# Ten weight tiles of its own and a second PSUM bank for the first stage of a decoder step

## The chip, the cores and the metric

The kernel runs on one core of a Trainium2 chip. The metric is the device time of one execution in microseconds; the time of a kernel is the median of its runs.

## What is computed

A step of a two-layer hybrid decoder on 256 prompt tokens and 8 sequences of 8 sample tokens (320 columns in all), all in fp32. Layer 0 mixes tokens by a gated MLP with a position-mixing matrix, layer 1 by a Mamba-2 scan; each is followed by a squared-ReLU MLP. Every sub-layer is normalised and then shifted and scaled by adaLN values, which are a projection of a conditioning vector. The first stage of the kernel covers the first lines of this cut:

```python
mod = (silu(c) @ ada_w[i] + ada_b[i]).reshape(c.shape[0], N_MOD, D_MODEL)
h = modulate(rms_norm(x, norm1_g[i]), mod[:, 0], mod[:, 1])   # h * (1 + scale) + shift
z = gelu(h @ w_in)
u, v = z[..., :D_GM], layer_norm(z[..., D_GM:], ln_g, ln_b)
...
y = (u * s) @ w_out
x = x + mod[:, 2][:, None, :] * y
h = modulate(rms_norm(x, norm2_g[i]), mod[:, 3], mod[:, 4])
x = x + mod[:, 5][:, None, :] * sq_relu_mlp(h, mlp_w1[i], mlp_w2[i])
```

D_MODEL is 1024, D_GM 2048; `c` holds 9 conditioning vectors (one for the prompt, eight for the samples).

## The kernel before

Activations lie with the model dimension on the partitions: `x`, `hhi` and `hlo` have 8 slices (`KD`) of 128 x 320. Every matrix product is made of three fp32r products: a weight tile is split into a high part `whi` (ScalarE, L135) and a low part `wlo` (VectorE, L136), the activations into `hhi` and `hlo`, and high x high, high x low and low x high are summed in PSUM. The split tiles rotate through three buffers each (`NHI`). Weights come in tiles of 128 x 1024 (512 KB), by SP's queue, into a ring `raw` of six (`NRAW`, L112) that all stages share.

The first stage (loop at L431) runs over the 8 slices `kt`. For each slice it makes the adaLN values of that slice and then adds the slice's part of the first half of `v = h @ w_in` to all its output tiles, in six PSUM banks that stay open through the loop (`acc0`, L424: three of the ring `mm`, the bank `nrm`, two of the three of the ring `ax`). In the order of the code a slice does this:

- it asks for the two halves of the next adaLN weights (`ada0`, L433), while the two of this slice, asked for a turn earlier, are used;
- L437: the adaLN product of a slice, for each half four matmuls of 128 x 32 against 128 x 256, each run as two instructions, so 8 instructions a half, summed in a bank from `ada_ps()` (L432), a ring of one;
- L445: load and split of the weights `gm_wv0` of the slice;
- L447: ScalarE copies the product out of PSUM; L450: four closing instructions on TensorE fold it and write it into the same bank; L453, L454: VectorE adds the bias and makes shift `md` and scale `am`;
- L456 to L463 and `norm_k` (L263): normalised, modulated and split slice `hhi`, `hlo`, and `hs` for the sample columns;
- `v_mm` (L407): 16 matmuls of 512 columns (L411 to L415).

At the end `v_out` (L417) takes the gelu of the six banks. The second stage (L471) does the same for the other half of `v`, with weights `gm_wv` through `wload` (L139). From there on each `wload` also takes a step of `ada_unit` (L152), which makes the adaLN values that later layers need: one load of `ada_w` (L156) and 8 instructions of L158, into the bank of `ada_ps()`. The projections of `u` and the rest of the kernel follow.

The norm of `x` at the start (L381 to L391) goes beside the first slices: its sum over the partitions is L210 on TensorE, its broadcast L205.

No order of instructions is written by hand across engines. A planner that simulates the program writes the order of each engine and of each DMA queue when the kernel is built; it takes what is ready and has a free buffer, earlier code first. So a load of a later stage can stand ahead of loads of this one on SP's queue. On the chip each engine and queue goes through its list in order, and waits at an instruction whose semaphores are not there yet.

Of the kernel before, what the change touches and what calls it, by code (L numbers as in the profile page):

```python
# [7 lines left out]
F32 = mybir.dt.float32  # L8
# [7 lines left out]
P = 128  # L16
# [6 lines left out]
T = TP + TS  # L23
# [15 lines left out]
NFIN = 5  # L39
MO = 6  # L40
NRAW = 6
NHI = 3
OFFS = (0, P, T - P)

# [7 lines left out]
def tile_trunk(ctx: ExitStack, tc: tile.TileContext, io):  # L52
# [14 lines left out]
    def nm(s):  # L67
        uid[0] += 1
        return f"{s}{uid[0]}"
# [3 lines left out]
    x = const.tile([P, KD, T], F32, name="x")  # L73
# [26 lines left out]
    def mm_ps():  # L100
        return psm.tile([P, 512], F32, tag="mm", name=nm("mm"))

    def ax_ps():
        return psx.tile([P, 512], F32, tag="ax", name=nm("ax"))

    def ada_ps():
        return psa.tile([P, 512], F32, tag="ada", name=nm("adap"))

    def nrm_ps():
        return psn.tile([P, 512], F32, tag="nrm", name=nm("nrm"))  # L110

    def raw_tile():  # L112
        return wp.tile([P, 8 * P], F32, tag="raw", name=nm("raw"), bufs=NRAW)

# [3 lines left out]
    b1 = lambda v: v.rearrange("p (b t) -> p b t", t=LS)  # L118
    bb = lambda v: v.unsqueeze(2).to_broadcast([P, NB, LS])

    # ---------------------------------------------------------------- weight stream and adaLN blocks
    fill = {"q": [], "rate": 0.0, "n": 0.0, "done": set()}

    def step():
# [7 lines left out]
    def split(raw, n=8 * P, eng=dve):  # L132
        hi = wp.tile([P, 8 * P], F32R, tag="whi", name=nm("whi"), bufs=NHI)
        lo = wp.tile([P, 8 * P], F32R, tag="wlo", name=nm("wlo"), bufs=NHI)
# [48 lines left out]
            dve.scalar_tensor_tensor(amul[2 * l + f // 3], md, 1.0, vec[:, g0 : g0 + 8].unsqueeze(2).to_broadcast([P, KD, 9]), ADD, MUL)  # L183
        fill["done"].add((l, f))

    # ---------------------------------------------------------------- norms
    def neg_rsqrt(r, v, a):
        dve.tensor_scalar(r.bitcast(I32), v.bitcast(I32), -0.5, 1597463007.0, MUL, ADD)
        for _ in range(3):
# [111 lines left out]
            act.activation(ghi[:, m, TP:T], t1, AF.Copy)  # L301
            pool.tensor_tensor(glo[:, m, TP:T], t1, ghi[:, m, TP:T].bitcast(F32), SUB)

    # ---------------------------------------------------------------- projections
    def mm3(ps, w, kk, hi, lo, first, last, n=T):
        whi, wlo = w
        pe.matmul(ps[:, :n], lhsT=whi[:, kk, :], rhs=hi, start=first, stop=False)  # L307
# [35 lines left out]
    def new_pool(side, bufs=1):  # L343
        c = ExitStack()
        return c, c.enter_context(tc.tile_pool(name=nm("pl"), bufs=bufs, side=side, reuse_waits="tile"))
# [29 lines left out]
        c.close()  # L375
        return ng

    # ---------------------------------------------------------------- layer 0 mixer
    fill["q"] = [ada_unit(l, f) for l in range(2) for f in range(6) if (l, f) not in ((0, 0), (0, 1), (1, 5))]
    act.activation(zero, zero, AF.Sqrt)  # L380
    for k in range(KD):  # L381
# [25 lines left out]
    def v_mm(pp, pq, whi, wlo, k):  # L407
        f, e = k == 0, k == KD - 1
        for c in range(2):
            sl = slice(c * P, (c + 1) * P)  # L410
            pe.matmul(pp[c], lhsT=hhi[:, k, sl], rhs=whi, start=f, stop=False)  # L411
            pe.matmul(pp[c], lhsT=hhi[:, k, sl], rhs=wlo, start=False, stop=False)  # L412
            pe.matmul(pp[c], lhsT=hlo[:, k, sl], rhs=whi, start=False, stop=e)  # L413
        pe.matmul(pq, lhsT=hs[:, k, :], rhs=whi, start=f, stop=False)
        pe.matmul(pq, lhsT=hs[:, k, :], rhs=wlo, start=False, stop=e)  # L415
# [6 lines left out]
        act.copy(vx[:, cs], pq)  # L422

    acc0 = [([mm_ps(), mm_ps()], ax_ps()), ([mm_ps(), nrm_ps()], ax_ps())]  # L424
    def load(src):
        raw = raw_tile()
        nc.sync.dma_start(raw, src)
        return raw

    nxt = [load(io["ada0"][0, hf]) for hf in range(2)]  # L430
    for kt in range(KD):  # L431
        ps = ada_ps()  # L432
        now, nxt = nxt, [load(io["ada0"][kt + 1, hf]) for hf in range(2)] if kt < KD - 1 else []  # L433
        for hf in range(2):
            raw = now[hf]
            for j in range(4):
                pe.matmul(  # L437
                    ps[32 * j : 32 * j + 32, :256],
                    lhsT=sc[:, 4 * hf + j, :],
                    rhs=raw[:, j * 256 : (j + 1) * 256],  # L440
                    start=(hf == 0),
                    stop=(hf == 1),
                    skip_group_check=True,
                )
        whi, wlo = split(load(io["gm_wv0"][kt]))  # L445
        sb = scratch()
        act.copy(sb[:, :256], ps[:, :256])  # L447
        pt = ps
        for i in range(2):
            pe.matmul(pt[:, 16 * i : 16 * i + 10], lhsT=sb[:, i * P : (i + 1) * P], rhs=cst[:, C_SS : C_SS + 10], start=True, stop=True, skip_group_check=True)  # L450
        for i in range(2):
            f = 8 * i + kt
            dve.tensor_scalar(md[:, f, :], pt[:, 16 * i : 16 * i + 9], vec[:, V_AB + f : V_AB + f + 1], None, ADD)  # L453
        dve.tensor_scalar(am[:, kt, :], md[:, 8 + kt, :], 1.0, vec[:, V_N1 + kt : V_N1 + kt + 1], ADD, MUL)  # L454
        t0 = tp.tile([P, TS], F32, tag="rs", name=nm("rs"))
        pool.tensor_tensor(b1(t0), b1(x[:, kt, TP:]), bb(am[:, kt, 1:9]), MUL)  # L456
        pool.tensor_tensor(t0, t0, r0[:, TP:], MUL)
        pool.tensor_tensor(b1(t0), b1(t0), bb(md[:, kt, 1:9]), ADD)
        act.activation(hhi[:, kt, TP:], t0, AF.Copy)
        dve.tensor_tensor(hlo[:, kt, TP:], t0, hhi[:, kt, TP:].bitcast(F32), SUB)  # L460
        norm_k(kt, am, md, r0)
        act.activation(hs[:, kt, 0:TS], t0, AF.Copy)
        act.activation(hs[:, kt, TS:], hlo[:, kt, TP:].bitcast(F32), AF.Copy)  # L463
        for j in range(2):
            cs = slice(512 * j, 512 * (j + 1))
            v_mm(*acc0[j], whi[:, cs], wlo[:, cs], kt)
    for j in range(2):
        v_out(j, *acc0[j])

# [80 lines left out]
    for m in range(KD):  # L550
        ps = proj1([io["gm_wo"][m, kc] for kc in range(2)], lambda k: uhi[:, k, :], lambda k: ulo[:, k, :])
        residual(ps, m, gate, g)
    uc.close()

    # ---------------------------------------------------------------- layer 0 mlp
    fill["rate"] = RATE1
    gc2 = []

# [5 lines left out]

    g = mlp(0, gc, g, nxt0)

    # ---------------------------------------------------------------- layer 1 mixer
    need(1, 4)
    fill["rate"] = 0.0
    r0 = rstd_x()  # L570
# [17 lines left out]
    ps = scaled(pss[0], r0)  # L588
# [52 lines left out]
        return st, bc, ea  # L641

    def ssd(g_, st, bc, ea, B, C, X, Z):
        # masked C.B^T and decays
        pc = ax_ps()
        for c in range(3):
            pe.matmul(pc[:, cq[c]], lhsT=B[:, OFFS[c] : OFFS[c] + P], rhs=C[:, cq[c]], start=True, stop=True, skip_group_check=True)
# [7 lines left out]
        dve.tensor_tensor(bc, bc, cbm.unsqueeze(1).to_broadcast([P, HG, T]), MUL)  # L655

        yield
        # token-major B and x
        Bd = dup(B, "dup0")
        Xd = [dup(X[r], f"dup{r + 1}") for r in range(2)]  # L660
        pB = ada_ps()
# [33 lines left out]
        dve.scalar_tensor_tensor(f2(xst), f2(xq), mrow(0), f2(xst).bitcast(F32), MUL, ADD)  # L695

        yield
        # prompt states
        pS = ax_ps()
        for c in range(2):  # L700
            pe.matmul(pS[:, c * GW : (c + 1) * GW], lhsT=Bn[:, c, :], rhs=xe[:, c, :], start=True, stop=True, skip_group_check=True)
# [4 lines left out]
        dve.tensor_tensor(fin, fin, pS[:, GW:], ADD)  # L706
        nc.gpsimd.dma_start(io["o_sp"][g_], fin)

        # terms of the entering states
        cp = mt([P, HG, P], "cp")  # L710
        cps = mt([P, NB, HG, LS], "cps")
        dve.tensor_tensor(cp, ea[:, :, :P], C[:, P:TP].unsqueeze(1).to_broadcast([P, HG, P]), MUL)
# [2 lines left out]
        for b in range(NB):  # L715
            j, hf = b % 4, b // 4
# [4 lines left out]
                start=True,  # L721
                stop=True,
# [3 lines left out]
        dve.tensor_tensor(ym, po.rearrange("p (c w) -> p c w", c=2), cst[:, C_DM : C_DM + GW].unsqueeze(1).to_broadcast([P, 2, GW]), MUL)  # L726

        yield
        # outputs of the scan
        Y = yt([P, 2, T], "Y")  # L730
        for r in range(2):
            py = ax_ps()
# [9 lines left out]
            for hf in range(2):  # L742
# [4 lines left out]
                    start=False,  # L747
                    stop=True,
# [4 lines left out]
        pool.tensor_tensor(Y, Y, Z, MUL)  # L753

        yield
        # gated group norm
        q0 = Z
        act.activation(q0, Y, AF.Square)
        q1 = scratch()
# [4 lines left out]
            dve.scalar_tensor_tensor(yst[m // 8][:, m % 8, :], Y[:, r], vec[:, V_NG + m : V_NG + m + 1], pr, MUL, MUL)  # L764

        yield
        # new sample states
        dec = ea[:, :, P:].rearrange("p h (b t) -> p b h t", t=LS)[:, :, :, LS - 1 : LS].to_broadcast([P, NB, HG, HD])
        pool.tensor_tensor(st.rearrange("p b (h e) -> p b h e", e=HD), st.rearrange("p b (h e) -> p b h e", e=HD), dec, MUL)
        for i in range(4):  # L770
# [24 lines left out]
    raw, dt, acm, stk, t1, t2, t3 = (yst[1][:, i, :] for i in range(7))  # L795
# [126 lines left out]
    acc["ring"] = nrm_ps  # L922
    yc.close()

    # ---------------------------------------------------------------- layer 1 mlp, final norm
    fill["q"].append(ada_unit(1, 5))
    fill["rate"] = 0.5
    mlp(1, gc, g, lambda: need(1, 5))
# [153 lines left out]
```

## Time and profile before

| | us |
|---|---|
| runs | 1133.29, 1131.8, 1141.0 |
| median | 1133.29 |
| span of the profiled execution | 1132.3 |

The span of the profiled execution goes from its first to its last instruction. The page gives busy time by engine: TensorE's matmuls 95% of the span, VectorE 62%, ScalarE 45%, GpSimd 35%. A matmul's busy time includes its way through the array, which overlaps that of the next, so these 95% are not TensorE at its peak; an idle time of TensorE is what counts. Of a wait the profile names who ended it, by the semaphore that came last. "PEclk" is the share of TensorE's full clock that was granted.

### The profile page before, as it was taken

To read this page: it belongs to the slowest core of one execution; us is meant where nothing else is said; L and a number is where in the kernel's file an instruction comes from. 1 tells how busy PE (TensorE), PEld (TensorE's weight loads), DVE (VectorE), ACT (ScalarE), POOL (GpSimd) and SP (SyncE) were. 2 spreads that over 40 slices of the span, in tenths; PEclk is the share of its full clock that TensorE was granted. 3 is DMA by queue.
4 is the path that set the end of the run, shared out by engine and by line. 5 is a ranking of instruction groups with operands and counts; after the bars stand their busy time and mean duration, and the time that the engine had idled before them with its cause. 6 is when DMAs were issued, how large, how long until landed. Compare 5 with 4: busy or idle time off the path is not lost.

```text
span 1132.3 us, 19072 instructions
## 1 busy us (share of the span) xinstructions
PE 1078.2 (95%) x7457; PEld 978.7 (86%) x7457; DVE 702.7 (62%) x1120; ACT 513.4 (45%) x899; POOL 395.3 (35%) x456
## 2 busy tenths in 40 slices
PE   5999999999999999999897999989999999999996
PEld 4667888889988898999895888888889999999996
DVE  3544856436644433446998999998976674443332
ACT  4443333435544433335773555554525555543331
POOL 1200124332333302223777666656423433320111
PEclk9999999999999999999998999998999999999998
DMA  9867785675767766445363555554345565444421
GB/s 342 295 224 248 272 299 166 208 245 183 233 213 223 220 211 222 149 149 181 98 206 115 191 190 182 183 183 137 132 157 188 173 232 165 150 151 149 149 94 47
DMA packets 60874, 213.92 MB, mean 189 GB/s; under 512 B 6560, under 2 KB 12128, under 8 KB 58480
## 3 DMA queue, kind: packets, MB, share of 16 engines
q1 hardware_dynamic: 58544, 200.47, 53.9%
q0 software_dynamic: 1952, 11.98, 2.8%
q8 instruction: 58, 0.95, 0.3%
q10 hardware_dynamic: 288, 0.26, 0.1%
q14 instruction: 32, 0.26, 0.1%
HBM read 199.31 MB, written 12.85 MB: 187 GB/s over the span
## 4 chain that ended last, share of the span: by engine, by line
PE 68%; DVE 18%; DMA 4%; issue 4%; POOL 2%; ACT 2%; SPq 0%; POOLq 0%; DVEq 0%; ACTq 0%
PE mm L307 18%; PE mm L309 17%; PE mm L308 17%; DVE co L615 5%; PE adap L158 4%; DVE wlo L136 2%; DVE nv L192 1%; PE mm L411 1%; PE mm L412 1%; DMA raw<-w_in 1%; PE mm L413 1%; PE ax L774 1%; PE ax L307 1%; ACT whi L135 1%; PE ax L308 1%
## 5 line engine op out<-in xcount | busy, mean ns | idle before, releaser
L136 DVE TENSOR_TENSOR wlo<-raw,whi 128x1024 fp32r<-128x1024 f32 (+1 forms) x221 | 272.3, 1233 | 216.9 <-ACT whi L135 216.0
L135 ACT ACTIVATE whi<-raw 128x1024 fp32r<-128x1024 f32 (+1 forms) x243 | 255.1, 1050 | 320.1 <-PE mm L308 213.8
L307 PE MATMUL mm<-hhi,whi 128*128 128x320 f32 x952 | 305.5, 321 | 2.3 <-ACT cb L608 1.8
L308 PE MATMUL mm<-hlo,whi 128*128 128x320 f32 x952 | 299.8, 315 | 1.3 <-DVE hlo L276 1.3
L309 PE MATMUL mm<-hhi,wlo 128*128 128x320 f32 x952 | 299.8, 315 | 1.3 <-DVE wlo L136 0.8
L307 PEld LDWEIGHTS mm<-hhi,whi 128*128 128x128 f32 x952 | 181.8, 191 | 20.4 <-issue 12.7
L308 PEld LDWEIGHTS mm<-hlo,whi 128*128 128x128 f32 x952 | 182.3, 191 | 3.4 <-DVE hlo L276 1.6
L309 PEld LDWEIGHTS mm<-hhi,wlo 128*128 128x128 f32 x952 | 181.6, 191 | 3.9 <-DVE wlo L136 1.4
L307 PE MATMUL mm<-mhi,whi 128*128 128x320 f32 x512 | 159.1, 311 | 0.0
L309 PE MATMUL mm<-mhi,wlo 128*128 128x320 f32 x512 | 158.1, 309 | 0.0
L308 PE MATMUL mm<-mlo,whi 128*128 128x320 f32 x512 | 157.9, 308 | 0.0
L358 POOL TENSOR_TENSOR ta<-ta 128x320 f32<-128x320 f32 x64 | 81.5, 1275 | 142.3 <-ACT ta L356 126.8
L307 PEld LDWEIGHTS mm<-mhi,whi 128*128 128x128 f32 x512 | 96.1, 188 | 4.1 <-issue 4.1
L308 PEld LDWEIGHTS mm<-mlo,whi 128*128 128x128 f32 x512 | 96.1, 188 | 0.0
L309 PEld LDWEIGHTS mm<-mhi,wlo 128*128 128x128 f32 x512 | 96.1, 188 | 0.0
L293 POOL TENSOR_TENSOR x<-x,rs 128x64 f32<-128x64 f32 x28 | 12.0, 430 | 226.5 <-DVE rs L292 226.5
L615 DVE SCALAR_TENSOR_TENSOR co<-cb,vec,co 128x344 f32<-128x344 f32 x96 | 82.3, 867 | 1.7 <-ACT co L613 1.2
L360 DVE TENSOR_TENSOR mlo<-ta,mhi 128x320 fp32r<-128x320 f32 x64 | 34.7, 547 | 53.6 <-ACT mhi L359 53.6
L359 ACT ACTIVATE mhi<-ta 128x320 fp32r<-128x320 f32 x64 | 30.1, 470 | 79.1 <-POOL ta L358 79.1
L136 POOL TENSOR_TENSOR wlo<-raw,whi 128x1024 fp32r<-128x1024 f32 x22 | 56.3, 2559 | 21.5 <-ACT whi L135 21.2
L158 PE MATMUL adap<-raw,sc 128*32 128x256 f32 x640 | 53.2, 392 | 0.9 <-DMA raw<-ada_w 0.9
L290 DVE SCALAR_TENSOR_TENSOR x<-mm,mod,x 128x256 f32<-128x256 f32 x29 | 14.0, 483 | 48.2 <-PE mm L309 46.8
(344 smaller groups left out, 1833.8 us busy)
## 6 DMA issues: line engine op xcount, KB each, us to landing
raw<-mlp_w SPq DMA_DIRECT2D x128, 512.0 KB, 3.9
raw<-ada_w SPq DMA_DIRECT2D x80, 512.0 KB, 4.4
raw<-w_in SPq DMA_DIRECT2D x48, 512.0 KB, 3.5
raw<-ada SPq DMA_DIRECT2D x16, 512.0 KB, 5.9
raw<-gm_wv SPq DMA_DIRECT2D x16, 512.0 KB, 6.2
raw<-gm_wu SPq DMA_DIRECT2D x16, 512.0 KB, 5.4
raw<-gm_wo SPq DMA_DIRECT2D x16, 512.0 KB, 4.5
st<-state SPq DMA_DIRECT2D x8, 1024.0 KB, 5.7
```

The costliest lines, as they stand in the source:

```text
L135: act.activation(hi[:, :n], raw[:, :n], AF.Copy)
L136: eng.tensor_tensor(lo[:, :n], raw[:, :n], hi[:, :n].bitcast(F32), SUB)
L158: pe.matmul(ps[32 * j : 32 * j + 32, :256], lhsT=sc[:, k, :], rhs=r[:, j * 256 : (j + 1) * 256], start=(k == 0), stop=(k == KD - 1), skip_ ...
L290: dve.scalar_tensor_tensor(x[:, m, :TP], ps[:, :TP], gate[:, m, 0:1], x[:, m, :TP], MUL, ADD)
L293: (dve if m == KD - 1 else pool).tensor_tensor(x[:, m, TP:], x[:, m, TP:], t0, ADD)
L307: pe.matmul(ps[:, :n], lhsT=whi[:, kk, :], rhs=hi, start=first, stop=False)
L308: pe.matmul(ps[:, :n], lhsT=whi[:, kk, :], rhs=lo, start=False, stop=False)
L309: pe.matmul(ps[:, :n], lhsT=wlo[:, kk, :], rhs=hi, start=False, stop=last)
L358: pool.tensor_tensor(s, t, t, MUL)
L359: act.activation(mhi[:, m, :], s, AF.Copy)
L360: dve.tensor_tensor(mlo[:, m, :], s, mhi[:, m, :].bitcast(F32), SUB)
L615: dve.scalar_tensor_tensor(o[:, :CO], cb[:, k : k + CO], wv(k), o[:, :CO], MUL, ADD)
```

## The change

- A pool of its own on the right side of SBUF holds ten tiles of 128 x 1024 for the first stage (`NRAW0`). Both the `ada0` and the `gm_wv0` loads of that stage go there, and no longer into the shared ring `raw` of six. The pool closes at the end of the stage.
- The adaLN product of a slice goes to the bank of `ada_ps()` for odd slices and to the third bank of the ring `ax` for even ones.
- The halves of a slice are multiplied in the order 1, 0, so the first matmul waits for the half that is asked for second, and `start` and `stop` change places.

Nothing is added to or taken from what is loaded or computed. Headings in comments are also left out.

```diff
@@ -39,6 +39,7 @@
 NRAW = 6
+NRAW0 = 10
 NHI = 3
...
@@ -422,24 +423,26 @@
     acc0 = [([mm_ps(), mm_ps()], ax_ps()), ([mm_ps(), nrm_ps()], ax_ps())]
+    s0, s0p = new_pool("right")
+
     def load(src):
-        raw = raw_tile()
+        raw = s0p.tile([P, 8 * P], F32, tag="raw0", name=nm("raw0"), bufs=NRAW0)
         nc.sync.dma_start(raw, src)
         return raw
 
     nxt = [load(io["ada0"][0, hf]) for hf in range(2)]
     for kt in range(KD):
-        ps = ada_ps()
+        ps = ada_ps() if kt % 2 else ax_ps()
         now, nxt = nxt, [load(io["ada0"][kt + 1, hf]) for hf in range(2)] if kt < KD - 1 else []
-        for hf in range(2):
+        for hf in (1, 0):
             raw = now[hf]
             for j in range(4):
                 pe.matmul(
                     ps[32 * j : 32 * j + 32, :256],
                     lhsT=sc[:, 4 * hf + j, :],
                     rhs=raw[:, j * 256 : (j + 1) * 256],
-                    start=(hf == 0),
-                    stop=(hf == 1),
+                    start=(hf == 1),
+                    stop=(hf == 0),
                     skip_group_check=True,
                 )
         whi, wlo = split(load(io["gm_wv0"][kt]))
...
             v_mm(*acc0[j], whi[:, cs], wlo[:, cs], kt)
+    s0.close()
     for j in range(2):
         v_out(j, *acc0[j])
```

## Rows read from the trace of the kernel before

**Rows 1.** The page: the span, and the chain that ended last by engine.
```profile
span 1132.3 us, 19072 instructions
PE 68%; DVE 18%; DMA 4%; issue 4%; POOL 2%; ACT 2%; SPq 0%; POOLq 0%; DVEq 0%; ACTq 0%
```

**Rows 2.** Stretches: length; busy PE, PEld, DVE, ACT, POOL; granted clock, DMA share, GB/s.
```profile
10.00:21.70 11.70, 10.68 (x55) 7.15 (x56) 4.34 (x14) 3.34 (x9) 1.83 (x3) 1.00 1.03 414
21.70:68.00 46.30, 42.89 (x287) 30.40 (x286) 24.93 (x55) 21.59 (x49) 10.61 (x21) 1.00 0.85 302
68.00:134.00 66.00, 66.00 (x408) 52.03 (x407) 41.14 (x69) 23.99 (x31) 4.70 (x3) 1.00 0.73 239
134.00:137.70 3.70, 2.35 (x18) 1.82 (x20) 3.50 (x7) 1.65 (x3) 0.00 (x0) 1.00 0.41 123
137.80:141.10 3.30, 3.30 (x18) 2.64 (x11) 1.85 (x3) 1.38 (x2) 0.00 (x0) 0.50 0.94 341
```

**Rows 3.** Waits of TensorE, 16 to 68 us: total us, times, longest.
```profile
PE mm L411 <- ACT hhi L266: 1.1, 1, 1.1
PE adap L437 <- PE adap L450: 1.1, 2, 0.6
PE adap L450 <- ACT ta L447: 0.9, 2, 0.5
PE adap L158 <- DMA raw<-ada_w: 0.9, 1, 0.9
```

**Rows 4.** Waits of SP's queue, 0 to 70 us.
```profile
SPq L427 <- PE adap L437: 19.2, 6, 5.3
...
SPq L513 <- DMA raw<-ada: 1.0, 1, 1.0
```

**Rows 5.** Timeline, 46 to 50 us: start, length, instruction, in brackets idle before.
```profile
46.51 0.51 PE L450 MATMUL adap<-cst,ta 128*128 128x10 f32 x4
...
47.52 1.07 PE L437 MATMUL adap<-raw,sc 128*32 128x256 f32 x16 [0.50 <-PE adap L450]
...
48.17 1.06 ACT L135 ACTIVATE whi<-raw 128x1024 fp32r<-128x1024 f32 x1 [3.83 <-DMA raw<-gm_wv]
...
49.26 1.23 DVE L136 TENSOR_TENSOR wlo<-raw,whi 128x1024 fp32r<-128x1024 f32 x1 [1.05 <-ACT whi L135]
...
49.67 0.51 PE L411 MATMUL mm<-whi,hhi 128*128 128x512 f32 x1 [1.09 <-ACT hhi L266]
```

**Rows 6.** Timeline of the start, 10 to 17 us, TensorE's adaLN and norm matmuls.
```profile
10.10 1.08 PE L437 MATMUL adap<-raw,sc 128*32 128x256 f32 x8 [10.10 <-DMA raw<-ada]
...
11.11 1.44 PE L210 MATMUL nrm<-ones_d,acc 128*128 128x1 f32 x6
...
12.48 1.08 PE L437 MATMUL adap<-raw,sc 128*32 128x256 f32 x8
...
16.77 1.93 PE L437 MATMUL adap<-raw,sc 128*32 128x256 f32 x16 [0.56 <-PE adap L450]
```

**Rows 7.** DMA, 3 to 25 us: packets, volume, mean rate.
```profile
DMA packets 2771, 8.67 MB, mean 394 GB/s; under 512 B 317, under 2 KB 487, under 8 KB 2771
```

**Rows 8.** Timeline of SP's queue, 7 to 12 us: issues.
```profile
7.86 0.33 SPq L492 DMA_DIRECT2D cst<-cst  x1
...
9.98 0.33 SPq L513 DMA_DIRECT2D lnb<-ln_b  x1
11.32 0.33 SPq L427 DMA_DIRECT2D raw<-ada  x1
```

**Rows 9.** Timeline of TensorE, 20 to 32 us, projection matmuls.
```profile
20.50 1.42 PE L412 MATMUL mm<-wlo,hhi 128*128 128x512 f32 x3
...
22.00 0.85 PE L413 MATMUL mm<-whi,hlo 128*128 128x512 f32 x3
...
31.39 0.97 PE L411 MATMUL mm<-whi,hhi 128*128 128x512 f32 x3
```

**Rows 10.** Waits of TensorE, 134 to 142 us.
```profile
PE ax L172 <- ACT adas L169: 1.3, 1, 1.3
```

## What the change will do

> **What bounds the kernel now.** I read the page first, for its span and its chain of waits [rows 1]. The span is 1132.3 us, 1.0 us under the median of the runs shown (1133.29), so I carry any change of the span over to that median one to one. TensorE holds 68% of the chain: the kernel is bound by the time in which TensorE issues matmuls, and a change that takes none away can only give back time in which TensorE stands still.
>
> So the second view is the busy time by stretch [rows 2]. The reader is to see three things. In the first stage as it runs at full rate, 21.7 to 68 us, TensorE is busy for 42.89 of 46.30 us, which leaves 3.4 us idle. In the stretch behind it, 68 to 134 us, it is busy for all 66.00 us: whatever the first stage gives back is passed on, for nothing there waits on anything but TensorE. And the first stage's DMA share of 0.85 says that transfers come close to their limit there without passing it.
>
> The third view is TensorE's waits in the first stage [rows 3]. They add up to 1.1 + 1.1 + 0.9 + 0.9 = 4.0 us, and they are what this change can reach: no row there reads "mm L411 <- DMA" or the like, so the first stage does not wait for the loads that it gets ten tiles for. The SP queue does wait, 19.2 us for adaLN matmuls to free a tile [rows 4], but that is the queue's own time.
>
> **The change part by part.**
>
> *The ten tiles.* The 24 loads of the stage (16 of ada0, 8 of gm_wv0) are as many and as large as before, with nothing added on the queue. They can be asked for earlier, as far ahead as 10 tiles. No TensorE wait on them exists, so the direct gain is nothing; what hides it now is that the data is there early enough. Indirectly the six tiles of the shared ring are free from the start, so the second stage's ada_w and gm_wv loads can come early. That takes away the wait of L158 for ada_w, 0.9 us [rows 3].
>
> *Two banks in turn.* Before, adaLN part kt+1 cannot start until VectorE has read part kt out of the one bank. That is the wait of L437 for L450, 1.1 us in two places [rows 3]. One of them can be followed [rows 5]: the closing matmuls L450 of the sixth part start at 46.51, the next part's L437 at 47.52 after 0.50 idle. The modulation of the sixth part, which L450 ends, is late with them, ScalarE takes a weight split first (48.17, 1.06 us), and the sixth projection starts only at 49.67 after 1.09 idle for hhi. With a second bank adaLN can run a part further ahead, so that hhi is made while the projection before it runs, and both waits go: 1.1 + 1.1 us. The wait of L450 for the copy L447 (0.9 us) is a latency inside one part: it goes where the planner finds other matmuls to put between, and stays where not. Its bounds are 0 and 0.9; I take the middle, 0.45, as nothing in the trace decides.
>
> The Trainium skill, "TensorE: Matmul & The Clock Gate", section "HAM oscillation — how this bites in real kernels", reports of one kernel that double-buffering PSUM brought nothing more (126.6 to 125.5 us there). This trace does not agree outright, since it has a wait on the bank of 1.1 us; by that rule the sum below would lose it, which is the first rival's case.
>
> *Halves together.* From the second part on all 16 instructions already run in one block (16.77, x16), so only the first part changes [rows 6]. Its first half ran from 10.10, L210 of the norm from 11.11 for 1.44 us, its second half from 12.48 to 13.56. Now the half that is loaded second goes first, so neither can start before that one lands. A half MB takes 1.33 us at 394 GB/s [rows 7], so that is about 10.10 + 1.33 = 11.4. With L210 ahead of them, to 12.55, and 1.93 us for the 16 at the early rate (the x16 row), the part ends at 14.5 against 13.56: 0.9 us late. With L210 behind them (11.4 + 1.93 + 1.44 = 14.8 against 12.55) the norm is 2.2 us late instead. Bounds 0 (if the modulation has slack) and 2.2; I take 0.9. What it delays is the first projection, and TensorE has to fill that time: it can, with an adaLN part that stood on its path later, 1.07 us by the block at 47.52 [rows 5], because a bank and a loaded tile are there. Of that I take half, 0.5, for whether it is put there is the planner's.
>
> *What moves on the queues.* Loads of later stages go ahead of first-stage loads when a tile is not free: the loads of L492, L512 and L513 stand between two of L427 (7.86 to 9.98, then 11.32) [rows 8], though they are used after the second stage. The shared ring adds up to six loads that can jump in like this. SP does not run away, since L513 waited 1.0 us for an ada tile's landing that it has no use for [rows 4]: issue goes at the pace of landings.
>
> *Sum.* Removed: 1.1 (bank) + 1.1 (hhi behind it) + 0.9 (ada_w) + 0.45 (copy) = 3.55; added at the start: 0.9 - 0.5 = 0.4. Net 3.15 us less: a span of 1129.1, and 1133.29 - 3.15 = 1130.1 us for the median. A measurement of this kernel can tell about 1% (11.3 us) from no change, so this counts as no change.
>
> **The rivals.**
>
> *Waits only move.* The bank wait comes back as a wait on the same chain L437, L447, L450, L453, L266, because the static order that the planner writes still puts L450 behind a projection; only the ada_w wait goes, and the start costs its 0.9: 1133.3. For it: hhi was late also because ScalarE was held by a split, which no bank changes [rows 5]. Against it: two of four rows of waits name the bank or follow from it. Spread 1132 to 1135.
>
> *Pulled-in loads starve the stage (slower).* If all nine foreign loads (six ring tiles, L492, L512, L513) go between the tenth and eleventh, that eleventh, gm_wv0 of the third part, lands at 10.10 + 19 x 1.33 = 35.4, and after its split (1.06) the projection can start at 36.5, against 31.39 before [rows 9]: 5.1 late. Without any it would land at 23.4 and be split at 24.5, so there is room for 6.9 us, five loads; it decides from the sixth on. TensorE covers some 1.4 with the next adaLN part (1.07 and its closing matmuls), leaving 3.7 of standstill. A standstill is followed by a dearer stretch: after 134 to 137.7 us, where TensorE was busy for 2.35 of 3.70, the clock was granted at 0.50, so 1.2 instead of 2.4 GHz, for 3.3 us [rows 2], and half of that, 1.7, is lost. 1130.1 + 3.7 + 1.7 = 1135.5. For it: the three loads that did jump. Against: issue at the pace of landings, which gives the ring time to free a tile in between.
>
> *Split buffers taken (slower by more).* A gm_wv tile of the second stage that lands early may be split early, and would hold one of the three whi/wlo buffers until 68 us. One taken costs nothing; with two taken, each of the six remaining projections waits for a split of 1.06 + 1.23 = 2.3 us behind the previous one [rows 5], of which adaLN work of 1.4 can cover some: 5.4 us to 13.8 us, or 1135.5 to 1143.9. It needs two such splits ahead of the stage's own.
>
> *A better start.* TensorE gives three L412 matmuls 1.42 us at 20.50 and three L413 of the same shape 0.85 us at 22.00 [rows 9]: before about 21.7 it ran at half rate, though the granted clock of that stretch reads 1.00 [rows 2]. If two parts are pulled into the gaps of the start and full rate comes one such stretch sooner, 1.1 + 1.7 us more are saved, and if the pause at 134 to 137.7 (1.3 us on L169 [rows 10]) with its slow stretch (1.7) shifts away as well, 3.0: 1130.1 - 5.8 = 1124.3.
>
> **How the numbers follow.** Chances: forecast 0.48 (1127 to 1132), waits only move 0.27, starved 0.13, buffers taken 0.04, better start 0.08. The forecast is the likeliest one's 1130.1. The range 1125.0 to 1136.5 covers all of the first two and most of the third and the last. Faster by over 1% (under 1122) needs more than every idle microsecond named: 0.03. Slower by over 1% (over 1144.6) needs the buffers taken with no cover, or standstills that I have not found: 0.04. Within 1%: 0.93.
>
> **What would show it.** Right: TensorE's waits from 16 us to the end of the first stage under 1.5 us, without rows of L437 on L450 and of L158 on ada_w; the first gelu (L420) some 3 us sooner than before, the first L411 at most 1 us later. Wrong: a wait of whi (L135) on raw0 with TensorE idle behind it between 28 and 36 us, a wait of L411 on whi, or ada_w loads ahead of first-stage loads on SP by more than five. The prediction fails if later stages, whose order is written anew too, move by more than these few microseconds.

## The result, and the profile after

The changed kernel takes 1140.08 us (median of 20 runs, 1132.95 to 1146.93), the kernel before 1131.38 us beside it (20 runs, 1125.83 to 1141.44). The ratio is 1.0071, with a 95% interval of 1.0048 to 1.0095: slower by 0.7%, which is within 1%, but on the other side of nothing than forecast and above the range. A second measurement of the same kernel, beside its own runs of before, gives 1.004 (1.0008 to 1.0073). The forecast started from 1133.29, the median of the 3 runs that it had of before. Runs over 1.5% above the fastest of their kernel are called slow: the ratios leave them out, the medians in the tables have them.

The profiled execution is the quickest of the 20, so its span lies under that of before [rows 1] although the median lies 8.7 us above. The totals therefore tell little here, and the two traces have to be compared by position. The page of after:

```profile
span 1131.2 us, 19059 instructions
...
PE 70%; DVE 18%; issue 4%; ACT 3%; POOL 2%; DMA 2%; POOLq 0%; DVEq 0%; ACTq 0%
```

TensorE's waits of after, 16 to 68 us (total, times, longest), stand against [rows 3]:

```profile
PE mm L412 <- ACT whi L136: 3.3, 1, 3.3
PE mm L412 <- ACT hhi L267: 1.4, 1, 1.4
```

Four rows of 4.0 us have become two of 4.7. The rows of L437 on L450, of L450 on its copy and of L158 on ada_w are gone. A wait on the weight split L136 stands in their place, which the kernel before did not have at all. The stretches of after, to be held against [rows 2] (length; busy PE, PEld, DVE, ACT, POOL; granted clock, DMA share, GB/s):

```profile
10.00:21.70 11.70, 9.60 (x58) 6.49 (x59) 5.10 (x17) 4.12 (x9) 1.91 (x5) 0.96 1.03 410
21.70:68.00 46.30, 43.00 (x265) 29.39 (x264) 21.42 (x47) 16.90 (x43) 12.58 (x20) 0.90 0.66 257
68.00:134.00 66.00, 64.89 (x386) 50.89 (x387) 39.39 (x67) 27.09 (x37) 4.70 (x3) 1.00 0.71 237
134.00:145.00 11.00, 10.00 (x76) 8.68 (x75) 8.94 (x16) 3.87 (x6) 0.00 (x0) 1.00 0.83 305
...
20.80:24.10 3.30, 3.30 (x9) 2.51 (x9) 2.84 (x6) 2.23 (x7) 1.87 (x3) 0.50 1.02 408
34.50:41.20 6.70, 5.08 (x12) 4.02 (x13) 4.02 (x8) 3.61 (x9) 2.45 (x4) 0.50 1.03 410
```

In 21.7 to 68 us TensorE is busy as long as before (43.00 against 42.89 us), but gets through 265 matmul records instead of 287: the clock is 0.90 in the mean, because in two stretches, 20.80 to 24.10 and 34.50 to 41.20 us, it is granted at 0.50, so at 1.2 GHz. Busy time alone would have hidden the loss. The DMA share fell from 0.85 to 0.66, but not evenly, as two further stretches of after show:

```profile
34.40:50.00 15.60, 13.88 (x76) 10.02 (x76) 7.05 (x15) 6.54 (x17) 4.00 (x7) 0.78 0.96 381
50.00:68.00 18.00, 18.00 (x125) 11.82 (x125) 10.70 (x22) 7.78 (x18) 5.96 (x9) 1.00 0.14 43
```

The queue is full to the end of the stage's loads and then has nothing to do, for the ring holds tiles that nobody uses yet (SP waits 18.1 us for one, up to 62.50). So the transfers came earlier, and not in the order in which they were needed. That order is in the timeline of SP's queue of after (start, length, issue), against [rows 8]:

```profile
9.47 1.62 SPq L430 DMA_DIRECT2D raw<-ada  x2
12.05 0.33 SPq L157 DMA_DIRECT2D raw<-ada_w  x1
13.33 0.33 SPq L147 DMA_DIRECT2D raw<-gm_wv  x1
14.61 0.33 SPq L157 DMA_DIRECT2D raw<-ada_w  x1
15.89 0.33 SPq L147 DMA_DIRECT2D raw<-gm_wv  x1
17.17 0.33 SPq L157 DMA_DIRECT2D raw<-ada_w  x1
18.45 0.33 SPq L147 DMA_DIRECT2D raw<-gm_wv  x1
19.80 0.33 SPq L430 DMA_DIRECT2D raw<-gm_wv  x1
```

After ten loads of the first stage come six for later stages, L157 and L147 in turn, into the six tiles of the shared ring. Only then comes the eleventh of the first stage, the gm_wv0 of the third slice. From issue to landing it took 11.5 us (line, issue, count, KB, us):

```profile
raw<-gm_wv SPq DMA_DIRECT2D x1, 512.0 KB, 11.5
```

It landed at 19.80 + 11.5 = 31.3 us. What that did on TensorE, in the timeline of after around it (in brackets the idle time before, and what ended it), against [rows 9]:

```profile
19.82 0.50 PE L412 MATMUL mm<-whi,hhi 128*128 128x512 f32 x1 [1.36 <-ACT hhi L267]
...
25.27 1.05 PE L440 MATMUL ax<-raw,sc 128*32 128x256 f32 x10
...
30.17 0.42 PE L440 MATMUL ax<-raw,sc 128*32 128x256 f32 x3
...
33.50 0.51 ACT L267 ACTIVATE hhi<-ta,mod 128x256 fp32r<-128x256 f32 x1 [1.35 <-DVE ta L266]
...
35.03 1.04 ACT L136 ACTIVATE whi<-raw 128x1024 fp32r<-128x1024 f32 x1
...
36.12 1.22 PE L412 MATMUL mm<-whi,hhi 128*128 128x512 f32 x2 [3.30 <-ACT whi L136]
```

The third projection starts at 36.12 us where it started at 31.39 before [rows 9]: 4.7 us late, 3.30 of them standstill. The landing at 31.3 does not set this time by itself. TensorE's order cuts the third adaLN part in two (10 of its 16 instructions at 25.27, the rest behind a projection, from 30.17). In ScalarE's order the copies and the hhi of that part stand ahead of the split, so the split starts only at 35.03, 3.7 us behind the landing. In a second trace of the same kernel (e0_again) the tile lands earlier, at 19.68 + 10.1 = 29.8, and the projection starts later, at 36.94. So on the chip the projection waited for the split's place in ScalarE's order, not for the tile. That this place goes back to the six loads is shown only further down, where they are held back.

The sum by position: 4.7 us late at 36 us, then half rate to 41.3 us (the trace has it from 34.4 us on, but TensorE stood still until 36.12), so 5.1 us of matmuls at half rate, of which half, 2.6, is lost. The first u projection, ahead of which both kernels have done the same work, starts 5.7 us later (before, then after):

```profile
100.17 0.31 PE L307 MATMUL mm<-hhi,whi 128*128 128x320 f32 x1
```
```profile
105.90 0.31 PE L308 MATMUL mm<-hhi,whi 128*128 128x320 f32 x1
```

So 4.7 + 2.6 - 5.7 = 1.6 us came back on the way. Behind the third projection the kernel before waits 3.0 us (1.1 for hhi, 0.9 for ada_w, and 0.5 of each of the other two rows), the changed one 1.1 us, for the gelu L421 at 74.19 (64.89 of 66.00 us busy in the row of 68 to 134 us). The 1.9 us between them would do.

Behind about 100 us every engine has the same order of instructions in both kernels, but for a few neighbours that change places. More comes back there by the clock: the half rate that the kernel before has behind 137.8 us [rows 2] is not there in after (1.00 in 134 to 145 us), though a wait for the adas copy stands in both (1.3 and 1.0 us). From 146 us on the changed kernel is 3.6 us late in this pair of profiles; why the medians lie further apart, here and in the shortened kernels below, stays open. Further on the clock differs in layer 1 (two stretches of after, columns as above):

```profile
538.00:625.00 87.00, 77.70 (x509) 72.41 (x510) 84.53 (x122) 58.11 (x124) 66.09 (x80) 0.94 0.45 150
625.00:784.00 159.00, 146.10 (x1023) 131.35 (x1021) 148.01 (x244) 82.26 (x151) 100.02 (x109) 0.94 0.53 176
```

The same two stretches in a second profile of the same kernel (e0_again, span 1142.0 us):

```profile
538.00:625.00 87.00, 75.34 (x480) 70.24 (x478) 80.65 (x116) 54.52 (x116) 64.29 (x78) 0.92 0.44 143
625.00:784.00 159.00, 144.15 (x1003) 129.62 (x1003) 145.79 (x241) 82.16 (x154) 94.47 (x107) 0.91 0.52 177
```

One kernel is granted 0.94 or 0.91 there from run to run. By an estimate from these rows that is 0.02 x 87 + 0.03 x 159 = 6.5 of the 10.8 us between the two profiles. The runs of either kernel spread over 14 to 20 us, more than the first stage could give.

### The profile page after: what moved, and what is told of

Read it like the earlier page. It is cut to its first block, busy times and chain, and to the rows that moved or that the text cites. A ratio compares the mean times of both kernels' runs of the same rounds, so it can differ in the third digit from the quotient of the medians.

```text
span 1131.2 us, 19059 instructions
## 1 busy us (share of the span) xinstructions
PE 1078.7 (95%) x7457; PEld 979.0 (87%) x7457; DVE 702.6 (62%) x1120; ACT 513.6 (45%) x899; POOL 397.8 (35%) x456
## 4 chain that ended last, share of the span: by engine, by line
PE 70%; DVE 18%; issue 4%; ACT 3%; POOL 2%; DMA 2%; POOLq 0%; DVEq 0%; ACTq 0%
PE mm L308 18%; PE mm L310 17%; PE mm L309 17%; DVE co L619 5%; PE adap L159 4%; DVE wlo L137 2%; PE mm L412 1%; PE mm L413 1%; PE mm L414 1%; DVE nv L193 1%; DVE bc L657 1%; PE ax L778 1%; PE ax L308 1%; ACT whi L136 1%; PE ax L309 1%
## 5 line engine op out<-in xcount | busy, mean ns | idle before, releaser
L136 ACT ACTIVATE whi<-raw 128x1024 fp32r<-128x1024 f32 (+1 forms) x243 | 254.9, 1050 | 311.4 <-PE mm L309 216.5
## 6 DMA issues: line engine op xcount, KB each, us to landing
raw<-ada SPq DMA_DIRECT2D x16, 512.0 KB, 10.1
```

What stands on the lines that cost most here:

```text
L136: act.activation(hi[:, :n], raw[:, :n], AF.Copy)
```

## The experiments

Three theories were set against each other. P: the loads of later stages, pulled ahead of the stage's own, starve it. S: the start and the order that the planner writes with two banks cost the time. C: there is no effect of the change, only the chance of the clock in layer 1. The change has three parts: A the pool of ten tiles, B the two banks, C' the order of the halves (1, 0).

**Full kernels, 5 rounds each.** First the changed kernel once more, A alone, and B with C' alone.

e0_again has no edit. 

> The changed kernel itself once more, beside the kernel before on the same chip, for a second profile. Theory P (pulled-in loads): six ring loads of the second stage go out ahead of the eleventh load of the first stage, the first stage ends some 5 to 6 us late again, with a TensorE wait of about 3 us on whi and half-rate stretches behind it; time 1.005 to 1.011 of before. Theory S (start and static order): the same time, but the loss sits ahead of 26 us and in late adaLN parts. Theory C (chance of the clock): the first-stage loss varies with the stretches at half rate, and the ratio is within 0.997 to 1.003.

e1_pool takes B and C' back:

```diff
-        ps = ada_ps() if kt % 2 else ax_ps()
+        ps = ada_ps()
-        for hf in (1, 0):
+        for hf in range(2):
```

> Only the pool of ten tiles: one PSUM bank for adaLN and the halves in the old order, as in the kernel before. Six ring loads still go out ahead of the eleventh first-stage load. Theory P: slower like the changed kernel, 1.004 to 1.010, first stage 4 to 6 us late. Theory S: as before, within 0.3%, since the start runs the halves as before.

e2_banks takes A back:

```diff
-        raw = s0p.tile([P, 8 * P], F32, tag="raw0", name=nm("raw0"), bufs=NRAW0)
+        raw = raw_tile()
```

> Only the two banks and the order of the halves: all loads of the first stage in the shared ring of six, so nothing of the second stage can be pulled in. Theory P: not slower, 0.996 to 1.001, with the bank waits (1.1 us) gone. Theory S: slower by 0.4 to 0.9%, with adaLN parts cut in two by projections and the first projection about 1 us late.

e3_hold keeps the whole change, but each load into the shared ring is issued behind the last load of the first stage:

```diff
     def load(src):
...
-        nc.sync.dma_start(raw, src)
+        hold[:] = [nc.sync.dma_start(raw, src)]
...
     def wload(src, eng=None):
         raw = raw_tile()
-        nc.sync.dma_start(raw, src)
+        with tc.issue_after(getattr(hold[0], "ins", hold[0])):
+            nc.sync.dma_start(raw, src)
```

and the same around the load in ada_unit. 

> The changed kernel with the loads of the shared ring queued behind the last load of the first stage on SP; the three loads of constants may still go between. Theory P: the loss is gone, 0.995 to 1.002 of before, the wait on whi near 32 to 36 us gone. Theory S: 1.004 to 1.010 still.

e4_poolhold is A with that hold, without B and C'. 

> The whole kernel with the pool of ten tiles, the ring's loads held behind the first stage's own, one adaLN bank and the halves in the old order. The shortened form gained 2.7 us over the shortened kernel before. If later stages keep it: 0.996 to 0.999 of before. If the spread of the later stages hides it: 1.000 within 0.3%.

full_Aholdall holds the loads of L496, L516 and L517 back as well. 

> The whole kernel with the pool of ten tiles, one adaLN bank, the old order of the halves, and all loads of later stages, constants too, held behind the stage's own. From the shortened form (261.4 us against 265.1): 3 to 4 us less than the kernel before, 0.9955 to 0.998. If the later stages take it back: 1.000 within 0.3%.

| kernel | median us | ratio to before (95%) |
|---|---|---|
| e0_again (A, B, C') | 1139.18 | 1.0040 (1.0008 to 1.0073) |
| e1_pool (A) | 1137.49 | 1.0039 (1.0012 to 1.0065) |
| e2_banks (B, C') | 1133.27 | 1.0020 (0.9990 to 1.0050) |
| e3_hold (A, B, C', hold) | 1136.38 | 1.0038 (1.0011 to 1.0065) |
| e4_poolhold (A, hold) | 1129.56 | 0.9966 (0.9934 to 0.9998) |
| full_Aholdall (A, all held) | 1129.63 | 0.9985 (0.9955 to 1.0016) |

What follows: the loss is repeated, so C alone does not hold. The pool alone has a loss of the size of the whole, and the same pool with the hold has none; e1_pool and e4_poolhold, each beside runs of before on its own chip, have intervals that do not meet. That is P. But e3_hold kept a loss with the loads held, so P alone does not do either. Intervals of about 0.3%, 3.4 us, are too wide to part the rest.

**Shortened kernels.** To take layer 1 and its clock out of the measurement, the kernel was ended behind the mixer of layer 0. Its order of instructions is the full kernel's up to there.

```diff
     uc.close()
+    gc.close()
+    for k in range(KD):
+        nc.sync.dma_start(io["o_y"][:, k, :], x[:, k, :])
```

Before, measured twice on one chip, and after:

> The kernel before, ended behind the mixer of layer 0: the MLPs, layer 1 and the final norm are left out and x is written as it stands, so this times the first 260 us or so alone, with the same order on every engine up to there. Base for the next three. All theories: one time, around 245 to 265 us, with a spread over its runs of a few us at most, against 15 to 20 us of the whole kernel.

> The shortened kernel before once more (MLPs, layer 1 and final norm left out): 265.1 us within 1 us if the shortened times of different jobs can be set side by side; if chips differ by more, the comparisons across jobs hold only to that difference.

> The changed kernel, ended at the same place (MLPs, layer 1 and final norm left out). Theory P and theory S both: 4 to 7 us over the shortened kernel before. Theory C, that the loss is chance of the clock or comes from later stages: under 2 us.

The parts, with the edits shown above:

> Only the pool of ten tiles, ended at the same place (MLPs, layer 1 and final norm left out). Theory P: 3 to 6 us over the shortened kernel before, since the six loads go ahead here as well. Theory S: within 1.5 us of it.

> The changed kernel with the ring's loads queued behind the first stage's last load, ended at the same place (MLPs, layer 1 and final norm left out). Theory P: no more than 1.5 us over the shortened kernel before, and 3 us or more under the shortened changed kernel. Theory S: as late as the shortened changed kernel.

> Only the two banks and the order of the halves, all loads of the stage in the shared ring of six, ended behind the mixer of layer 0 (MLPs, layer 1 and final norm left out). The shortened kernel before took 265.1 us, the changed one 272.3, the pool alone 267.2, the changed one with the ring's loads held back 266.7. Theory P+S (the pulled-in loads make TensorE wait, and the adaLN part cut in two by a projection makes the wait longer): 263 to 266 us, with no stretch at half rate behind 30 us. Theory S alone: 267 us or more.

> The pool of ten tiles alone, with the ring's loads held behind the stage's own, ended at the same place (the rest left out). Theory P: the 2.1 us of the pool alone go, 263 to 265.5 us, and with them the wait of adaLN for ada0 (2.5 us) and the 6.8 us at half rate behind it. If the pool costs something by itself (its place in SBUF, longer queues): 267 us again.

> Pool, one bank, old order, and the three loads of constants held back too; ended at the same place (the rest left out). If those three cost nothing in the middle of the stage, since ten tiles cover them: 262.4 us within 0.7. If they cost: 260 to 261.5 us.

cut_ABhold has the old order of the halves, cut_AChold the one bank:

> Pool, held loads and two banks, halves in the old order; ended behind the mixer of layer 0 (MLPs, layer 1 and final norm left out). If the banks cost the 4.3 us (adaLN of the second slice goes ahead of the first projection and the third part is cut in two): 265.5 to 267.5 us. If the order of the halves does: 262 to 263.5 us.

> Pool, held loads and the halves in the new order, one bank; ended at the same place (the rest left out). If the banks cost the 4.3 us: 262.5 to 264 us, the start alone 0.5 to 1 us late. If the order of the halves does: 265.5 to 267.5 us.

In cut_pipeAfter and cut_pipe the projection of a slice is written one turn later, behind the next adaLN part, so that this part is not cut; cut_pipe also holds all later loads back:

```diff
+        pend.append((whi, wlo, kt))
+        if kt:
+            proj()
-        for j in range(2):
-            cs = slice(512 * j, 512 * (j + 1))
-            v_mm(*acc0[j], whi[:, cs], wlo[:, cs], kt)
...
+    proj()
```

> The changed kernel with the projection of a slice written one turn later in the code, so that the planner no longer cuts the third adaLN part in two around a projection; the six ring loads still go ahead. Ended at the same place (the rest left out). Theory P (loads alone): 270 to 273 us as before this edit, since gm_wv0 of the third slice lands no sooner. Theory S (cut part): 264 to 267 us. Both at work: 267 to 270 us.

> The changed kernel with the projection a turn later in the code and with all loads of later stages, the three of constants too, held behind the stage's own; ended at the same place (the rest left out). Both theories: the best of all, 261 to 264.5 us, as no TensorE wait of over 1.5 us is left after the start.

| kernel | parts | median us | lowest to highest |
|---|---|---|---|
| cut_before, cut_before2 | none | 265.10, 265.18 | 264.20 to 267.03, 261.75 to 266.60 |
| cut_after | A, B, C' | 272.31 | 270.90 to 272.81 |
| cut_pool | A | 267.20 | 265.63 to 267.28 |
| cut_banks | B, C' | 266.64 | 265.38 to 268.17 |
| cut_hold | A, B, C', hold | 266.73 | 265.23 to 268.88 |
| cut_Ahold | A, hold | 262.38 | 261.49 to 263.80 |
| cut_Aholdall | A, all held | 261.42 | 260.73 to 262.87 |
| cut_ABhold | A, B, hold | 268.08 | 265.38 to 271.51 |
| cut_AChold | A, C', hold | 269.27 | 264.41 to 271.02 |
| cut_pipeAfter | A, B, C', projection later | 270.58 | 268.59 to 271.90 |
| cut_pipe | A, B, C', projection later, all held | 266.11 | 264.89 to 267.76 |

Several expectations missed. e2_banks (1.0020), e3_hold (1.0038), cut_banks (266.6) and cut_pool (2.1 us above before) lie between what the two theories said. cut_pipe was named the best of all at 261 to 264.5 us and took 266.1. full_Aholdall (0.9985) lies above its 0.998, which leaves its other case, no effect within 0.3%. cut_ABhold and cut_AChold lie above both of their forecasts; the medians of the runs that their ratios use are 267.1 and 266.4 us, each in the range given for the case that the part in it costs.

Two limits hold for what follows. cut_ABhold, cut_AChold and cut_Aholdall ran on another chip than the rest, with no shortened kernel before beside them; the whole kernel before took 1133.5 us there, and 1131.4 to 1134.6 us on the chip of the others. And each edit makes the planner write a new order, so the price of a part is that of the order to which it led.

*The loss lies in the first 265 us.* The change costs 7.1 us here (265.2 to 272.3), as the full kernels' 0.4 to 0.7% had it (4.5 to 8 us), and the ranges do not touch. The two profiled executions end only 4.5 us apart (spans of 265.2 and 269.7; that of cut_before is its slowest). The delay is there by the first u projection, in the timelines of cut_before, cut_after and cut_Ahold:

```profile
100.33 0.31 PE L307 MATMUL mm<-hhi,whi 128*128 128x320 f32 x1
```
```profile
106.26 0.31 PE L308 MATMUL mm<-hhi,whi 128*128 128x320 f32 x1
```
```profile
96.91 0.31 PE L311 MATMUL mm<-hhi,whi 128*128 128x320 f32 x1
```

*The pulled-in loads cost about 5 us.* With the pool alone 262.4 becomes 267.2 (4.8), with the whole change 266.7 becomes 272.3 (5.6). In cut_pool it is another load that comes late, an ada0 tile that is issued at 26.59, behind the six ring loads and the three of constants. It took 10.7 us to land, and here TensorE waits for the landing itself. The SP queue, the timeline of TensorE, and the stretch behind the standstill:

```profile
20.15 0.33 SPq L147 DMA_DIRECT2D raw<-gm_wv  x1
21.48 0.33 SPq L430 DMA_DIRECT2D raw<-ada  x1
...
26.59 0.33 SPq L430 DMA_DIRECT2D raw<-ada  x1
```
```profile
37.34 1.08 PE L440 MATMUL adap<-raw,sc 128*32 128x256 f32 x8 [2.47 <-DMA raw<-ada]
```
```profile
36.90:43.70 6.80, 5.81 (x21) 4.13 (x22) 2.70 (x6) 2.09 (x5) 1.45 (x3) 0.50 1.03 412
```

2.47 us of standstill and half of the 5.81 us in which TensorE was busy at half rate are 5.4; measured were 4.8. In cut_hold, where the six loads are held back, the third split starts at 26.18 us as its tile lands, and the third projection at 34.32, with one more adaLN part done ahead of it; in cut_after they start at 35.54 and 36.63. So the loads cost the time in either kernel, in cut_pool by a landing, in the changed kernel by the order that the planner wrote around them. Why it set the split so late is not shown.

*The pool without them gains 2.7 us.* 265.1 becomes 262.4 (the fastest of the ten runs of before, 261.75, lies within the range of cut_Ahold). With the constants held back too it is 261.4, which the ranges do not tell from 262.4. The hold without the pool was not measured, so the gain is that of both together. The waits of TensorE, 16 to 68 us, in cut_before and then in cut_Ahold:

```profile
PE mm L411 <- ACT hhi L266: 1.7, 1, 1.7
PE adap L158 <- DMA raw<-ada_w: 1.3, 1, 1.3
PE adap L437 <- PE adap L450: 1.1, 2, 0.6
PE adap L450 <- ACT ta L447: 0.9, 2, 0.5
```
```profile
PE mm L415 <- ACT hhi L270: 0.7, 1, 0.7
PE adap L443 <- PE adap L456: 0.6, 1, 0.6
```

5.0 us fall to 1.3, with one bank and the old order of the halves. Of the waits for the bank and for hhi, 1.1 + 1.7 us, 0.6 + 0.7 are left. [rows 5] have what joins these waits to the loads: ScalarE stood 3.83 us for a gm_wv tile, and its split then held up hhi. The view of all engines of before, 16 to 68 us, sums this up:

```profile
ACT whi L135 <- DMA raw<-gm_wv: 9.3, 5, 3.8
```

In cut_Ahold, with the tiles there earlier, this row is gone.

*The banks and the halves take the gain back.* With A and the hold, B and C' bring 262.4 to 266.7 (+4.3, ranges apart). Alone they bring 265.1 to 266.6 (+1.5, ranges overlapping). Part of the place is the start. The stretch from 20 to 24 us in cut_before, cut_Ahold, cut_banks, cut_hold, cut_ABhold and cut_AChold, in this order (the number behind PE's busy time is that of matmul records):

```profile
20.00:24.00 4.00, 4.00 (x29) 2.99 (x31) 1.31 (x5) 1.11 (x2) 0.59 (x2) 1.00 1.03 410
```
```profile
20.00:24.00 4.00, 4.00 (x21) 3.06 (x23) 2.23 (x5) 0.26 (x1) 0.30 (x1) 1.00 1.03 414
```
```profile
20.00:24.00 4.00, 4.00 (x10) 3.13 (x11) 2.07 (x8) 2.65 (x8) 1.31 (x4) 1.00 1.03 417
```
```profile
20.00:24.00 4.00, 4.00 (x11) 3.20 (x12) 3.54 (x9) 2.38 (x8) 2.41 (x4) 0.59 1.03 408
```
```profile
20.00:24.00 4.00, 4.00 (x10) 3.13 (x10) 3.61 (x9) 2.66 (x8) 1.88 (x3) 1.00 1.03 409
```
```profile
20.00:24.00 4.00, 3.75 (x9) 2.98 (x10) 1.71 (x2) 1.56 (x4) 0.00 (x0) 1.00 1.02 388
```

TensorE is busy in all of them or nearly so, but where banks or halves are new it gets through 9 to 11 matmuls instead of 21 to 29. Short adaLN matmuls in the one kernel and long projection matmuls in the other account for a part of this, half rate for the rest: in cut_hold the first projection's matmuls follow each other at 0.43 us until 23.1, where at full rate it is 0.23. In cut_hold TensorE runs both adaLN parts and the norm first, then waits 1.8 us for hhi, and starts the projection at 19.92, against 18.09 in cut_Ahold. The changed kernel shows how that comes about: with a second bank the second adaLN part goes ahead of the closing matmuls of the first, for which the first hhi waits. Before (first fence) and after:

```profile
15.23 0.97 PE L450 MATMUL adap<-cst,ta 128*128 128x10 f32 x4
```
```profile
15.41 1.94 PE L440 MATMUL adap<-raw,sc 128*32 128x256 f32 x16
...
17.28 0.64 PE L453 MATMUL ax<-cst,ta 128*128 128x10 f32 x4
```

The start is not all of it. cut_hold is through the first projection at 25.35 us and cut_Ahold at 23.83, 1.5 us apart, but their first u projections start at 100.68 and 96.91, 3.8 apart. The other 2.3 us lie in between, with as many matmul records (425) and no more waiting (0.6 against 0.7 us). There cut_Ahold runs the six remaining adaLN parts in one block of 16 instructions each, cut_hold only two of them, the rest in pieces. That the pieces cost the 2.3 us is not shown.

cut_ABhold and cut_AChold suggest that either part by itself loses the gain; their ranges, 6 us wide, don't tell which loses more. That stays open.

*The cut part is worth 1.7 us at most.* cut_pipeAfter leaves the loads ahead and does not cut the third part: 270.6 against 272.3, with ranges that overlap. The tile lands at 20.80 + 10.1 = 30.9, the split stands behind the third part's hhi again and starts at 35.02, and the third projection still starts at 36.11:

```profile
36.11 1.65 PE L412 MATMUL mm<-whi,hhi 128*128 128x512 f32 x3 [1.89 <-ACT whi L136]
```

Even with every load held and the projection a turn later (cut_pipe, 266.1), the two banks with the new order of the halves do not come under the kernel before.

## Why the prediction was wrong

The forecast was one for a kernel whose loads arrive in the order in which they are needed. Two steps failed. The larger is the last of the parts, **what moves on the queues**: "SP does not run away, [...] issue goes at the pace of landings", which should give the ring time to free a tile in between. So the sum had no term for it. Issues do go at the pace of landings, one in 1.28 us in the rows of SP above; but the pace decides nothing, the written order does. It was fixed by the planner, and it put all six ring loads ahead of the eleventh; that cost 4.8 us with the pool alone and 5.6 with the whole change. The second is the **two banks**: a gain of 2.2 us in the sum, with 0.4 lost by the halves, where both together measured a loss of 4.3 us once the tiles were there early. With the loads held back the changed kernel is still slower than before (e3_hold, 1.0038). Step by step:

- **Ten tiles, direct gain nothing:** wrong, and hidden. With the ring's loads held they are worth 2.7 us (cut_Ahold). The argument, no wait of TensorE on a load, looked at one engine's rows only. ScalarE did wait for loads, 9.3 us, 3.83 of them in [rows 5] right ahead of the split that the prediction names as holding up hhi, so a part of the waits on the bank and on hhi was the loads'.
- **Wait for ada_w gone, 0.9:** right; the row is not there in after.
- **Bank and hhi, 1.1 + 1.1:** mis-sized. The rows of L437 on L450 are gone as forecast, but 1.4 us of waiting for hhi stand at the first projection, and banks with halves together measured +1.5 us alone (ranges overlapping) and +4.3 us with pool and hold, not -2.2. The Trainium skill ("TensorE: Matmul & The Clock Gate", "HAM oscillation — how this bites in real kernels") reports of one kernel that double-buffered PSUM brought nothing more. Here no gain was measured either, with the order of the halves changed too (e2_banks 1.0020, 0.9990 to 1.0050).
- **Copy wait, 0.45 of 0.9:** the row is gone in after, so the upper bound was the better value; against the rest it is small.
- **Halves together, 0.9 late, 0.5 given back:** 1.2 late at the first projection (19.82 against 18.63), nothing given back there. Both kernels run two adaLN parts ahead of the first projection, so there was none to pull in; what changed is that the first part's closing matmuls came behind the second part (17.28 against 15.23). The half rate lasted to about 24.2 us instead of 21.7.
- **The starved rival** had the cause, six or more ring loads ahead: it named six as the number from which it decides, and six stood ahead. It gave 35.4 us for the landing with nine ahead, measured was 31.3 with six; by its 1.33 us a load, six give 10.10 + 16 x 1.33 = 31.4. That its projection at 36.5 meets the measured 36.12 is luck, since the split did not follow the landing. Its standstill was 3.7 against 3.30 measured, and its half-rate loss 1.7 against 2.6. It came out at 1135.5 because it started from a forecast that kept all gains; with its own two terms (3.7 + 1.7) on top of 1133.29 it would have stood at 1138.7, 5.4 us above before; the first u projection was 5.7 late, and the shortened kernels measured 7.1. Its chance of 0.13 was too low: its one counter-argument was the pace of SP.
- **Split buffers taken** did not occur: no split of a later stage held up the stage's own in the waits above. **A better start** did not either; the start is worse. One part of this rival did come, the half rate behind 137.8 us that is gone in after.
- **What would show it:** the first gelu was to be 3 us sooner; it starts at 73.54 against 65.14, 8.4 us later. Of the signs named for a wrong forecast these were there: a wait of TensorE on whi, six ring loads ahead (three of them ada_w), TensorE idle between 28 and 36 us. Not there was a wait of whi on raw0: the split came late by its place in ScalarE's order.

The version that beats both is the pool with the hold, one bank, and the halves as before: e4_poolhold with 0.9966 (0.9934 to 0.9998). With the constants held too it is 0.9985 (0.9955 to 1.0016), so 2 to 4 us, at the edge of what can be told.

## What to carry to other kernels

When a stage gets buffers of its own, the buffers it leaves are free from the first instant, and a planner fills them with loads that nobody needs yet: write down the new order of the queue, and hold later loads behind the last of the stage. A wait on a buffer or a bank in a stage fed just in time may be the feed's wait; look at what the other engines wait for, deepen the feed first and look at the row again. For a loss smaller than the run's spread, cut the kernel behind the changed stage and measure that.

## What the runs showed of the hardware

- A standstill of TensorE cost about as much again in clock. Matmuls ran at half rate for 5.1 us behind 3.30 us (after, clock 0.50), for 6.4 us behind 2.47 us (cut_pool, clock 0.50), and behind 1.89 us (cut_pipeAfter) matmuls of 128x512 took 0.63 instead of 0.40 us until about 39.4 us, some 3.3 us. About half of such a stretch is lost (matmuls 0.43 instead of 0.23 us apart). Shorter waits did not always do this: before has a half-rate stretch of 3.3 us behind a wait of 1.3 us at 134 to 137.7, after has none behind 1.0 us at the same place.
- A load of half a MB issued behind others on a full DMA took 9.9 to 11.5 us to land in after, at about 410 GB/s, where the medians of before between 13 and 40 us were 4.5 us for ada0 and 6.5 us for gm_wv0. SP's issues, which go at the pace of landings, stand 1.28 us apart there, so that the six loads from 12.05 us on put the eleventh at 19.80.
- The granted clock of a stretch can read 1.00 while the matmuls run at half rate: cut_banks reads 1.00 in 20 to 24 us, but spaces its matmuls at 0.43 us as cut_hold does at a clock of 0.59; the clock records of the cut_banks trace begin only at 24.7 us. At the start of a run the spacing of equal matmuls is the better sign.
